# Softmax of four heads in one tile, one multiplication by the reciprocal sums, and FFN activations at another address

## The chip, the cores and the metric

One Trainium2 chip, of which the kernel uses one core. The metric is the time of one execution on the device in microseconds (us), the median of several runs. The engines are named as the profile names them: PE is TensorE (PEld its weight loads), DVE is VectorE, ACT is ScalarE, POOL is GpSimd, SP is SyncE, which issues the transfers.

## The reference

The program chains two stacks of layers on one sequence of 256 tokens of width 1024. The first stack has two layers (a recurrent mixer, a gated linear attention, each with a convolutional FFN). The second, which the change touches, has four layers; each is FFN, mixer, FFN, with a LayerNorm behind each of the three. The mixers are DSA, FoX, MLA and DSA again, all with 16 heads and causal softmax. Cut to what matters:

```
for i in range(4):
    x = layer_norm(ALPHA * x + 0.5 * swiglu(x, ffn1_w13[i], ffn1_w2[i]), ...)
    y = (dsa, fox, mla)[i % 3] mixer of x      # softmax attention, 16 heads, then @ w_out[i]
    x = layer_norm(ALPHA * x + y, ...)
    x = layer_norm(ALPHA * x + 0.5 * swiglu(x, ffn2_w13[i], ffn2_w2[i]), ...)

p = softmax(where(mask, q @ k.T * scale, -inf))   # per head
o = p @ v
```

DSA makes its mask with an indexer: eight small heads, a relu of their products, a weighted sum, and the 64 best keys of each query.

## The kernel before

Every product of an activation with a weight runs as three matmuls in fp32r: both are split into a high and a low part (`hi`, `lo`), and hi x hi, hi x lo, lo x hi are added up in PSUM (`mm_b`, lines 438 to 440: the activation is the stationary operand, 512 columns of weights move; `mm_a`, lines 445 to 447: the weight is stationary, 256 tokens move). Weights come from HBM in pieces of 512 KB; ACT casts the high part (line 371), DVE subtracts it for the low part (line 372).

In the second stack the tokens lie in two halves of 128, t = 0 and 1, each a Python generator that yields after every piece of weights. They run interleaved, and both use a piece while it is there. Tile's scheduler, from its own estimate of each instruction's duration and not by hand, sets the order in which each engine's instructions stand; each engine then works its list in that order. The middle part of an FFN (`ffn_both`) takes both halves at once.

An attention (`attend`) handles one group g of four heads of one half; four groups, two halves and four layers make 32 of them. Half 1 sees 256 keys, half 0 sees 128 (nk). The steps:
- line 1221: PE makes the scores of the four heads in two PSUM banks.
- line 1226: DVE adds the mask, scales and takes the maximum of each head (in the trace a custom instruction and a read of its accumulator); line 1228: ACT takes exp with that maximum as bias, in place in the head's tile `s`, with the row sum in one column of `sm`.
- line 1231: DVE takes the reciprocal `rc` of the four sums; line 1233: one multiplication by a scalar for each head.
- line 1240: PE transposes the probabilities in blocks of 128x128; line 1241: DVE copies the first two heads' transposes to `pT`, ACT the other two's; line 1248: PE multiplies with `v`.
- `split` (lines 450 and 451) makes `oThi` and `oTlo`, the stationary operands of the output projection, which follows when all four groups of a half are through (`groups`). While half 1 is still in its attentions, the output projection of half 0 is what PE has to do in between. It ends in half 0's LayerNorm (`ln`, lines 1075 to 1084: residual sum, statistics, aggregate, normalise, scale and shift; the reciprocal root `rstd` comes from POOL, lines 420 and 423).

Other users of the names that are touched: `hidden` (lines 1105 to 1108) makes the FFN's gated activation in `th`, which is split or transposed and split into `hT` (`ht`, from the tag kT), the stationary operand of the down projection; `dsa_index` makes the relu of the indexer in `rl`. `s`, `th` and `rl` share the tag `s1k`, with five buffers of 1 KB per partition. `pad` allocates a tile that nobody uses, to move the addresses behind it.

Of the kernel before, what the change touches and what calls it, by code (L numbers as in the profile page):

```python
# [8 lines left out]
F32 = mybir.dt.float32  # L9
F32R = mybir.dt.float32r  # L10
I32 = mybir.dt.int32
AF = mybir.ActivationFunctionType
OP = mybir.AluOpType
# [240 lines left out]
class _Cols:  # L254
    def __init__(self):
        self.at, self.parts, self.n = {}, [], 0
# [794 lines left out]
class Block2:  # L1051
    def __init__(self, k):
        self.k, self.nc, self.a, self.P, self.Q = k, k.nc, k.a, k.P, k.Q
        self.V, self.ACT = k.nc.vector, k.nc.scalar
        self.padded = False
        self.gbt, self.shared, self.v, self.vt = {}, {}, [None, None], {}

    def gb(self, i):
# [43 lines left out]
    def hidden(self, u, v, n):  # L1102

        V = self.V
        th = self.Q.tile([128, n], F32, name="th", tag="s1k", bufs=5)
        self.ACT.activation(out=th, in_=u, func=AF.Tanh, scale=0.5)
        V.scalar_tensor_tensor(out=th, in0=th, scalar=1.0, in1=u, op0=OP.add, op1=OP.mult)
        V.tensor_tensor(out=th, in0=th, in1=v, op=OP.mult)  # L1108
        return th

    def ht(self, key, c):

        if not self.hT:
            self.k.pad(self.Q, "h", 24)
        if (key, c) not in self.hT:
            self.hT[key, c] = self.Q.tile([128, 2, 2, 256], F32R, name="hT", tag="kT", bufs=4)
        return self.hT[key, c]
# [93 lines left out]
    def attend(self, t, g, qh, kh, v, mask, scale, oT):  # L1211


        k, Q, V, ACT, nc = self.k, self.Q, self.V, self.ACT, self.nc
        nk = 128 * (t + 1)
        sm = k.small("sm", 4)

        sp = [k.bank("u", 4, (128, 2, 256)) for _ in range(2)]
        scores = [sp[e % 2][:, e // 2, :nk] for e in range(4)]
        for e in range(4):  # L1220
            nc.tensor.matmul(scores[e], qh(e), kh(e), start=True, stop=True)  # L1221
        probs = []
        for e in range(4):
            s = Q.tile([128, 256], F32, name="s", tag="s1k", bufs=5)[:, :nk]
            nb = k.small(f"nb{e}")
            V.tensor_tensor_reduce(out=s, in0=scores[e], in1=mask[:, :nk], scale=-scale, scalar=3.0e38,
                                   op0=OP.add, op1=OP.min, accum_out=nb)
            ACT.activation(out=s, in_=s, func=AF.Exp, scale=-1.0, bias=nb, accum_out=sm[:, e:e + 1])
            probs.append(s)
        rc = k.small("rc", 4)  # L1230
        V.reciprocal(out=rc, in_=sm)
        for e in range(4):
            V.tensor_scalar(out=probs[e], in0=probs[e], scalar1=rc[:, e:e + 1], scalar2=None, op0=OP.mult)
        pTs = []
        for e0 in (0, 2):
            pt = k.bank("u", 4, (128, 2, 2, 128))
            pT = Q.tile([128, 2, 2, 128], F32, name="pT", tag="pT", bufs=2)
            for e in range(2):
                for j in range(t + 1):
                    nc.tensor.transpose(pt[:, e, j, :], probs[e0 + e][:, j * 128:j * 128 + 128], k.ident)  # L1240
            (ACT.copy if e0 else V.tensor_copy)(out=pT[:, :, :t + 1, :], in_=pt[:, :, :t + 1, :])
            pTs.append(pT)

        op = k.bank("u", 4, (128, 2, 128))
        for e0 in (0, 2):
            for j in range(t + 1):
                for e in range(2):
                    nc.tensor.matmul(op[e * 64:e * 64 + 64, e0 // 2, :], v[j][:, e0 + e, :], pTs[e0 // 2][:, e, j, :],  # L1248
                                     start=j == 0, stop=j == t)
        if not oT:  # L1250
            if not self.padded:
                k.pad(Q, "o", 16)
                self.padded = True
            oT += [Q.tile([128, 8, 128], F32R, name=f"oT{p}", tag=f"oT{p}{t}", bufs=1) for p in ("hi", "lo")]
        k.split(oT[0][:, g * 2:g * 2 + 2, :], oT[1][:, g * 2:g * 2 + 2, :], op)

# [36 lines left out]
    def dsa_index(self, t, i, xT):  # L1293

        k, Q, V, ACT, nc = self.k, self.Q, self.V, self.ACT, self.nc
        sh = self.shared.setdefault(i, {})
        nk = 128 * (t + 1)
        if t == 0:
            sh["kiT"] = Q.tile([128, 256], F32, name="kiT", tag="kiT", bufs=1)
        kiT = sh["kiT"]  # L1300
        ki = Q.tile([128, 2, 64], F32, name="ki", tag="ki", bufs=2)
        wi = Q.tile([128, 8], F32, name="wi", tag="wi", bufs=2)
        qi = Q.tile([128, 8, 64], F32, name="qi", tag="s2k", bufs=2)
        r = []
        for q, nm in enumerate("si"):
            yield from self.proj(t, f"mx{i}.{nm}", xT, 8, r)
            ACT.copy(out=qi[:, q * 4:q * 4 + 4, :], in_=r[q][:, :256].rearrange("p (h d) -> p h d", h=4))
            if q == 0:
                ACT.copy(out=ki[:, 0, :], in_=r[0][:, 256:320])
                self.rope(t, ki[:, 0:1, :16], 8, 0)  # L1310
                V.tensor_copy(ki[:, 1, :], ki[:, 0, :])
            else:
                ACT.activation(out=wi, in_=r[1][:, 256:264], func=AF.Copy, scale=8.0 ** -0.5)
        self.rope(t, qi[:, :, :16], 8, 0)
        p = k.bank("u", 4)
        nc.tensor.transpose(p[:, :128], ki.rearrange("p a d -> p (a d)"), k.ident)
        ACT.copy(out=kiT[:, t * 128:t * 128 + 128], in_=p[:, :128])
        qiT = Q.tile([128, 4, 128], F32, name="qiT", tag="s2k", bufs=2)
        self.transposes(qi.rearrange("p (a b) d -> p a (b d)", b=2), 4, 128, qiT)
        sc = Q.tile([128, nk], F32, name="sc", tag=f"sc{t}", bufs=1)  # L1320
        for h in range(8):
            if h % 4 == 0:
                dp = [k.bank("u", 4, (128, 2, 256)) for _ in range(2)]
                for q in range(4):
                    r = slice(q % 2 * 64, q % 2 * 64 + 64)
                    nc.tensor.matmul(dp[q % 2][:, q // 2, :nk], qiT[r, (h + q) // 2, :], kiT[r, :nk], start=True, stop=True)
            rl = Q.tile([128, 256], F32, name="rl", tag="s1k", bufs=5)
            ACT.activation(out=rl[:, :nk], in_=dp[h % 2][:, h % 4 // 2, :nk], func=AF.Relu, scale=0.125)
            if h == 0:
                V.tensor_scalar(out=sc[:, :nk], in0=rl[:, :nk], scalar1=wi[:, 0:1], scalar2=None, op0=OP.mult)  # L1330
            else:
                V.scalar_tensor_tensor(out=sc[:, :nk], in0=rl[:, :nk], scalar=wi[:, h:h + 1], in1=sc[:, :nk], op0=OP.mult, op1=OP.add)
        cm = self.cmask[:, 128 - t * 128:256]
        V.tensor_tensor(out=sc[:, :nk], in0=sc[:, :nk], in1=cm, op=OP.add)
        for r in range(8):
            m8 = k.small("m8", 8)
            V.max(out=m8, in_=sc[:, :nk])
            V.match_replace(out=sc[:, :nk], in_to_replace=m8, in_values=sc[:, :nk], imm_value=-3.0e30)
        mask = Q.tile([128, nk], F32, name="dmask", tag=f"dm{t}", bufs=1)
        V.tensor_scalar(out=mask[:, :nk], in0=sc[:, :nk], scalar1=-2.0e30, scalar2=NEG, op0=OP.is_ge, op1=OP.mult)  # L1340
        V.tensor_tensor(out=mask[:, :nk], in0=mask[:, :nk], in1=cm, op=OP.add)
        return mask
# [226 lines left out]
```

## Time and profile before

| | us |
|---|---|
| median of 3 runs | 2665.33 (2660.8 to 2668.5) |
| the profiled execution, its own time | 2664.02 |
| its span, first to last instruction | 2662.2 |
| PE busy | 2598.1 |
| DVE busy | 1919.3 |
| ACT busy | 1413.6 |

The times of rows are us from the start of the span. PE's matmuls overlap, so a matmul's own duration (0.39 us for 512 columns) is longer than the distance from its start to the next one's (0.23 us); the second is what PE takes for it. The granted clock of PE was 0.995 over the span, its upper level.

### The profile page before, as it was taken

How to read it: one execution, taken by the hardware profiler on the slowest of the kernel's cores; microseconds unless marked ns; L12 is line 12 of the kernel's file. 1: busy time of each engine (PE TensorE's matmuls, PEld its weight loads, DVE VectorE, ACT ScalarE, POOL GpSimd, SP SyncE). 2: the span in 40 equal slices, each digit the busy share in tenths (PEclk: the TensorE clock that was granted, in tenths of full speed). 3: DMA queues.
4: the chain of work that ended last, by engine and by line, in shares of the span. 5: the costliest groups of instructions: out<-in, count | busy, mean ns of one | idle time of the engine just before them, and what ended most of it. 6: DMA issues, size and time to landing. Idle time of an engine off the chain costs nothing.

```text
span 2662.2 us, 44260 instructions
## 1 busy us (share of the span) xinstructions
PE 2598.1 (98%) x16680; PEld 2287.7 (86%) x16680; DVE 1919.3 (72%) x3876; ACT 1413.6 (53%) x2848; POOL 75.3 (3%) x115
## 2 busy tenths in 40 slices
PE   7899999999999999999999999999999999999998
PEld 5688977899899778989987899899889989977897
DVE  6889879887666877576666856766885676687765
ACT  4565564765544655445456544544654454456542
POOL 0000010000000000000000000000000000000000
PEclk9999999999999999999999999999999999999999
DMA  8868764664664536656654565664445565453652
GB/s 317 297 230 293 243 226 164 224 217 159 225 191 151 183 122 226 191 184 206 193 179 125 183 192 180 214 190 154 166 163 194 183 206 190 160 182 126 213 191 96
DMA packets 141081, 514.39 MB, mean 193 GB/s; under 512 B 16177, under 2 KB 16561, under 8 KB 139330
## 3 DMA queue, kind: packets, MB, share of 16 engines
q1 hardware_dynamic: 140866, 511.56, 57.9%
q8 instruction: 131, 2.15, 0.3%
q14 instruction: 84, 0.69, 0.1%
HBM read 510.44 MB, written 1.05 MB: 192 GB/s over the span
## 4 chain that ended last, share of the span: by engine, by line
PE 78%; issue 8%; DVE 7%; DMA 3%; ACT 2%; POOL 1%; DVEq 0%; SPq 0%; POOLq 0%; ACTq 0%
PE u L445 11%; PE u L446 11%; PE u L447 11%; PE y L438 10%; PE y L440 10%; PE y L439 10%; PE u L438 3%; PE u L439 3%; PE u L440 3%; DVE lo L372 2%; DMA raw<-w 2%; DMA adar<-ada 1%; PE u L1221 1%; PE u L469 1%; PE u L1248 1%
## 5 line engine op out<-in xcount | busy, mean ns | idle before, releaser
L372 DVE TENSOR_TENSOR lo<-raw,hi 128x512 fp32r<-128x512 f32 (+4 forms) x1501 | 1081.1, 746 | 497.0 <-ACT hi L371 484.5
L371 ACT CAST hi<-raw 128x512 fp32r<-128x512 f32 (+4 forms) x1501 | 952.1, 667 | 730.3 <-issue 413.5
L445 PE MATMUL u<-hThi,hi 128*128 128x256 f32 x3016 | 840.1, 279 | 2.4 <-ACT hi L371 1.4
L447 PE MATMUL u<-hThi,lo 128*128 128x256 f32 x3016 | 837.0, 278 | 0.6 <-DVE lo L372 0.6
L446 PE MATMUL u<-hTlo,hi 128*128 128x256 f32 x3016 | 837.5, 278 | 0.0
L445 PEld LDWEIGHTS u<-hThi,hi 128*128 128x128 f32 x3016 | 567.7, 188 | 7.1 <-DVE mn L916 1.6
L446 PEld LDWEIGHTS u<-hTlo,hi 128*128 128x128 f32 x3016 | 567.6, 188 | 4.7 <-issue 1.0
L447 PEld LDWEIGHTS u<-hThi,lo 128*128 128x128 f32 x3016 | 569.1, 189 | 1.2 <-DVE lo L372 1.0
L440 PE MATMUL y<-hi,hT 128*128 128x512 f32 x704 | 278.2, 395 | 0.0
L438 PE MATMUL y<-hi,hT 128*128 128x512 f32 x704 | 277.8, 395 | 0.0
L439 PE MATMUL y<-lo,hT 128*128 128x512 f32 x704 | 277.7, 394 | 0.0
L438 PE MATMUL y<-hi,hThi 128*128 128x512 f32 (+6 forms) x504 | 190.1, 378 | 3.5 <-ACT hThi L450 3.3
L439 PE MATMUL y<-lo,hThi 128*128 128x512 f32 (+6 forms) x504 | 186.3, 371 | 0.1
L440 PE MATMUL y<-hi,hTlo 128*128 128x512 f32 (+6 forms) x504 | 185.3, 372 | 0.2 <-DVE hTlo L451 0.2
L440 PEld LDWEIGHTS y<-hi,hT 128*128 128x128 f32 x704 | 132.6, 188 | 30.7
L438 PEld LDWEIGHTS y<-hi,hT 128*128 128x128 f32 x704 | 132.6, 188 | 28.3
L439 PEld LDWEIGHTS y<-lo,hT 128*128 128x128 f32 x704 | 132.6, 188 | 28.3
L438 PE MATMUL u<-hi,hThi 128*128 128x512 f32 x320 | 126.9, 398 | 4.9 <-ACT hThi L450 4.9
L450 ACT CAST hT<-th 128x256 fp32r<-128x256 f32 x144 | 58.4, 405 | 130.5 <-DVE th L1108 130.5
L439 PE MATMUL u<-lo,hThi 128*128 128x512 f32 x320 | 125.4, 393 | 0.0
L440 PE MATMUL u<-hi,hTlo 128*128 128x512 f32 x320 | 124.1, 394 | 0.0
L438 PEld LDWEIGHTS y<-hi,hThi 128*128 128x128 f32 x504 | 95.2, 189 | 21.4 <-ACT hThi L450 5.1
(301 smaller groups left out, 3119.3 us busy)
## 6 DMA issues: line engine op xcount, KB each, us to landing
raw<-w SPq DMA_DIRECT2D x823, 512.0 KB, 3.9
adar<-ada SPq DMA_DIRECT2D x80, 512.0 KB, 4.9
gb<-lngb SPq DMA_DIRECT2D x12, 1024.0 KB, 4.9
adag<-ada SPq DMA_DIRECT2D x8, 512.0 KB, 5.7
adag<-adag SPq DMA_DIRECT2D x8, 512.0 KB, 6.0
raw<-w SPq DMA_DIRECT2D x8, 384.0 KB, 2.9
raw<-w SPq DMA_DIRECT2D x5, 480.0 KB, 3.6
raw<-w SPq DMA_DIRECT2D x4, 396.0 KB, 2.9
```

The source lines that it names most:

```text
L371: nc.scalar.copy(out=hi[:, a:b], in_=r[:, a:b])
L372: nc.vector.tensor_tensor(out=lo[:, a:b], in0=r[:, a:b], in1=hi[:, a:b].bitcast(F32), op=OP.subtract)
L438: mm(out, xhi, w[0], start=start, stop=False)
L439: mm(out, xhi, w[1], start=False, stop=False)
L440: mm(out, xlo, w[0], start=False, stop=stop)
L445: mm(out, whi, xhi, start=start, stop=False)
L446: mm(out, whi, xlo, start=False, stop=False)
L447: mm(out, wlo, xhi, start=False, stop=stop)
L450: self.nc.scalar.copy(out=hi, in_=src)
L469: self.nc.tensor.transpose(p[:, k * 128:k * 128 + 128], x[:, (h + k) * 128:(h + k + 1) * 128], self.ident)
L1221: nc.tensor.matmul(scores[e], qh(e), kh(e), start=True, stop=True)
L1248: nc.tensor.matmul(op[e * 64:e * 64 + 64, e0 // 2, :], v[j][:, e0 + e, :], pTs[e0 // 2][:, e, j, :], start=j == 0, stop=j == t)
```

## The change

The four tiles `s` of a head become one tile `s4` of four heads and nk keys for each half (tags s40 and s41, one buffer each); the heads' slices of it are what reductions, exp and transposes use. The four multiplications by a scalar become one multiplication of two tensors, in which `rc` is broadcast along the keys. The tag s1k keeps `th` and `rl` and has two buffers. The pad ahead of `hT` shrinks from 24 to 8 floats and the pad ahead of `oT` is gone.

```diff
     def hidden(self, u, v, n):
-        th = self.Q.tile([128, n], F32, name="th", tag="s1k", bufs=5)
+        th = self.Q.tile([128, n], F32, name="th", tag="s1k", bufs=2)
...
     def ht(self, key, c):
         if not self.hT:
-            self.k.pad(self.Q, "h", 24)
+            self.k.pad(self.Q, "h", 8)
...
-        probs = []
+        s4 = Q.tile([128, 4, nk], F32, name="s", tag=f"s4{t}", bufs=1)
+        probs = [s4[:, e, :] for e in range(4)]
         for e in range(4):
-            s = Q.tile([128, 256], F32, name="s", tag="s1k", bufs=5)[:, :nk]
             nb = k.small(f"nb{e}")
-            V.tensor_tensor_reduce(out=s, in0=scores[e], in1=mask[:, :nk], scale=-scale, scalar=3.0e38,
+            V.tensor_tensor_reduce(out=probs[e], in0=scores[e], in1=mask[:, :nk], scale=-scale, scalar=3.0e38,
                                    op0=OP.add, op1=OP.min, accum_out=nb)
-            ACT.activation(out=s, in_=s, func=AF.Exp, scale=-1.0, bias=nb, accum_out=sm[:, e:e + 1])
-            probs.append(s)
+            ACT.activation(out=probs[e], in_=probs[e], func=AF.Exp, scale=-1.0, bias=nb, accum_out=sm[:, e:e + 1])
         rc = k.small("rc", 4)
         V.reciprocal(out=rc, in_=sm)
-        for e in range(4):
-            V.tensor_scalar(out=probs[e], in0=probs[e], scalar1=rc[:, e:e + 1], scalar2=None, op0=OP.mult)
+        V.tensor_tensor(out=s4, in0=s4, in1=rc[:, :, None].to_broadcast([128, 4, nk]), op=OP.mult)
...
         if not oT:
-            if not self.padded:
-                k.pad(Q, "o", 16)
-                self.padded = True
...
-            rl = Q.tile([128, 256], F32, name="rl", tag="s1k", bufs=5)
+            rl = Q.tile([128, 256], F32, name="rl", tag="s1k", bufs=2)
```

The addresses in a partition follow from the sizes of the tiles in the order of their first use. Modulo 256 bytes, the weights `hi` and `lo` stay at 224 and the activations `hThi` and `hTlo` at 160; `hT` goes from 96 to 32, `oThi` and `oTlo` from 224 to 96.

The order of the engines changes inside the four mixers only; those of the FFNs and of the first stack are as they were. In the changed kernel lines 1057 to 1220 are one lower, and the attention's are 1220 (scores), 1225, 1227 (exp), 1229 (reciprocal), 1231 (multiplication), 1238, 1239, 1246. The transposes of 1240 stand in 32 rows of PE's order in place of 50, the products of 1248 in 33 rows in place of 40.

DVE at the last attention (g = 3) of half 1 in layer 0, before, from the last reduction on; `x_70` is half 0's residual stream, `dmask` the mask:

```order
L1226 ISA s,nb_10152<-u,dmask 128x256
L1226 ISA nb_10152 128x1
L1075 SCALAR_TENSOR_TENSOR x_70<-x_70,y 128x512 x2
L1231 RECIPROCAL rc<-sm 128x4
L1076 BN_STATS bnst<-x_70 128x6
L1233 TENSOR_SCALAR s<-s,rc 128x256 x4
L1076 BN_STATS bnst<-x_70 128x6
L1241 COPY pT<-u 128x512
L1078 BN_AGGR bnmv<-bnst 128x2
```

The same place on DVE, after:

```order
L1225 ISA s,nb_10106<-u,dmask 128x256
L1225 ISA nb_10106 128x1
L1077 BN_AGGR bnmv<-bnst 128x2
L1080 SCALAR_TENSOR_TENSOR x_70<-x_70,bnmv,gb 128x1024
L1229 RECIPROCAL rc<-sm 128x4
L1083 SCALAR_TENSOR_TENSOR x_70<-x_70,rstd,gb 128x512
L1231 TENSOR_TENSOR s<-s,rc 128x1024
L1083 SCALAR_TENSOR_TENSOR x_70<-x_70,rstd,gb 128x512
L372 TENSOR_TENSOR lo_10336<-raw,hi_10335 128x512
L1239 COPY pT<-u 128x512
```

The residual sums and statistics of half 0 (1075 and 1076) have moved ahead of the reductions, and the aggregate, the normalisation and half of the scaling stand between the reductions and the multiplication.

PE at the same place, before, from the last matmuls of the output projection ahead of the transposes on:

```order
L438 MATMUL y<-hi_10051,oThi 128x512
L439 MATMUL y<-lo_10052,oThi 128x512
L1240 MATMUL u<-ident,s 128x128 x2
L440 MATMUL y<-hi_10051,oTlo 128x512
L1240 MATMUL u<-ident,s 128x128 x6
L438 MATMUL y<-hi_10051,oThi 128x512
L439 MATMUL y<-lo_10052,oThi 128x512
L440 MATMUL y<-hi_10051,oTlo 128x512
L438 MATMUL y<-hi_10196,oThi 128x512
L1248 MATMUL u<-pT,v 64x128 x8
```

And after:

```order
L438 MATMUL y<-hi_10147,oThi 128x512
L439 MATMUL y<-lo_10148,oThi 128x512
L440 MATMUL y<-hi_10147,oTlo 128x512
L1238 MATMUL u<-ident,s 128x128 x8
L1246 MATMUL u<-pT,v 64x128 x8
L469 MATMUL u<-ident,x_70 128x128 x4
L438 MATMUL y<-hi_10167,oThi 128x512
```

Between the scores and the first transpose stood 17 matmuls of the output projection and now stand 15; between the transposes and the products with v stood four and now none.

DVE at the attention g = 2 of half 1 in the MLA layer, before, from the last reduction on:

```order
L1226 ISA s,nb_20661<-u,cmask 128x256
L1226 ISA nb_20661 128x1
L1231 RECIPROCAL rc<-sm 128x4
L1233 TENSOR_SCALAR s<-s,rc 128x256 x4
L1075 SCALAR_TENSOR_TENSOR x_70<-x_70,y 128x512
L1241 COPY pT<-u 128x512
```

And after:

```order
L1225 ISA s,nb_20525<-u,cmask 128x256
L1225 ISA nb_20525 128x1
L1074 SCALAR_TENSOR_TENSOR x_70<-x_70,y 128x512
L1075 BN_STATS bnst<-x_70 128x6
L1229 RECIPROCAL rc<-sm 128x4
L1077 BN_AGGR bnmv<-bnst 128x2
L372 TENSOR_TENSOR lo_20811<-raw,hi_20810 128x512
L1231 TENSOR_TENSOR s<-s,rc 128x1024
L1080 SCALAR_TENSOR_TENSOR x_70<-x_70,bnmv,gb 128x1024
L1239 COPY pT<-u 128x512
```

A residual sum, statistics, an aggregate and a low part have come ahead of the multiplication, and the normalisation ahead of the copy. On PE there stood 13 matmuls of the output projection between these scores and the first transpose, and now 7; five stood between the transposes and the products with v, and now none.

## Rows read from the trace of the kernel before

**Rows 1.** The page: busy time by engine, and the chain that ended last, by engine.
```profile
PE 2598.1 (98%) x16680; PEld 2287.7 (86%) x16680; DVE 1919.3 (72%) x3876; ACT 1413.6 (53%) x2848; POOL 75.3 (3%) x115
PE 78%; issue 8%; DVE 7%; DMA 3%; ACT 2%; POOL 1%; DVEq 0%; SPq 0%; POOLq 0%; ACTq 0%
```
**Rows 2.** What PE waited for: line, waited for, us in total, times, longest.
```profile
PE u L1240 <- DVE s L1233: 4.6, 6, 1.8
```
**Rows 3.** Groups of PE's matmuls: line, tiles, shape, count, busy, mean ns, idle.
```profile
L440 PE MATMUL y<-hi,hT 128*128 128x512 f32 x704 | 278.2, 395 | 0.0
...
L438 PE MATMUL y<-hi,oThi 128*128 128x512 f32 x128 | 52.9, 414 | 0.0
```
**Rows 4.** PE's timeline: first and last matmul of an hT and an hThi stretch.
```profile
835.33 0.39 PE L438 MATMUL y<-hi,hT 128*128 128x512 f32 x1
...
857.40 0.39 PE L440 MATMUL y<-hi,hT 128*128 128x512 f32 x1
...
2156.63 0.40 PE L439 MATMUL u<-lo,hThi 128*128 128x512 f32 x1
...
2166.71 0.40 PE L438 MATMUL u<-hi,hThi 128*128 128x512 f32 x1
```
**Rows 5.** Groups on DVE, by shape: count, busy us, mean ns, idle before.
```profile
L1233 DVE TENSOR_SCALAR s<-s,rc 128x256 f32<-128x256 f32 x64 | 18.2, 349 | 0.4
L1233 DVE TENSOR_SCALAR s<-s,rc 128x128 f32<-128x128 f32 x64 | 14.0, 282 | 0.5
...
L372 DVE TENSOR_TENSOR lo<-raw,hi 128x512 fp32r<-128x512 f32 x1291 | 849.9, 686 | 463.3 <-ACT hi L371 452.8
L372 DVE TENSOR_TENSOR lo<-raw,hi 128x1024 fp32r<-128x1024 f32 x180 | 217.9, 1219 | 33.7 <-ACT hi L371 31.7
```
**Rows 6.** Timelines of DVE (first row) and PE, layer 0, half 1, g = 3.
```profile
984.50 0.42 DVE L1226 CUSTOM_DVE_ANT_0 s<-u,dmask 128x256 f32<-128x256 f32 x1 [1.39 <-PE u L1221]
...
984.40 0.50 PE L438 MATMUL y<-hi,oThi 128*128 128x512 f32 x1
984.75 0.40 PE L439 MATMUL y<-lo,oThi 128*128 128x512 f32 x1
...
988.21 0.39 PE L439 MATMUL y<-lo,oThi 128*128 128x512 f32 x1
988.56 0.41 PE L1240 MATMUL u<-ident,s 128*128 128x128 f32 x2
```
**Rows 7.** PE's timeline right behind them, around the products of pT and v.
```profile
990.40 0.40 PE L438 MATMUL y<-hi,oThi 128*128 128x512 f32 x1
990.73 1.09 PE L1248 MATMUL u<-pT,v 128*64 128x128 f32 x16
991.75 0.50 PE L439 MATMUL y<-lo,oThi 128*128 128x512 f32 x1
992.09 0.40 PE L440 MATMUL y<-hi,oTlo 128*128 128x512 f32 x1
```
**Rows 8.** Timelines of DVE and PE, MLA layer, half 1, g = 3; idle in brackets.
```profile
1950.43 0.42 DVE L1226 CUSTOM_DVE_ANT_0 s<-u,cmask 128x256 f32<-128x256 f32 x1
...
1954.18 0.75 DVE L1084 SCALAR_TENSOR_TENSOR x<-x,rstd,gb 128x512 f32<-128x512 f32 x1 [0.67 <-POOL rstd L423]
1954.85 1.14 DVE L1233 TENSOR_SCALAR s<-s,rc 128x256 f32<-128x256 f32 x4
...
1953.16 0.39 PE L440 MATMUL y<-hi,oTlo 128*128 128x512 f32 x1
1955.35 1.15 PE L1240 MATMUL u<-ident,s 128*128 128x128 f32 x8 [1.80 <-DVE s L1233]
```
**Rows 9.** The same in the MLA layer at g = 2.
```profile
1940.01 0.42 DVE L1226 CUSTOM_DVE_ANT_0 s<-u,cmask 128x256 f32<-128x256 f32 x1 [1.72 <-PE u L1221]
...
1942.81 1.14 DVE L1233 TENSOR_SCALAR s<-s,rc 128x256 f32<-128x256 f32 x4
...
1943.31 1.15 PE L1240 MATMUL u<-ident,s 128*128 128x128 f32 x8
```

More of the change, by code (lines that the diff above doesn't have):

```diff
@@ L1054, in __init__ @@
         self.V, self.ACT = k.nc.vector, k.nc.scalar
-        self.padded = False
         self.gbt, self.shared, self.v, self.vt = {}, {}, [None, None], {}
```

## The prediction

> **What bounds the kernel now.** I read the page first: TensorE (PE) is busy for 98% of the span and holds 78% of the chain that ended last, so time moves only where PE gets slower steps, fewer steps, or a wait [rows 1]. Next the list of what PE waited for: at the changed place, L1240 (transposes of the probabilities) behind DVE's normalisation L1233, it lost 4.6 us in 6 waits, the longest 1.8 us [rows 2]. So there is little waiting to win; the question is what new waiting appears, and whether PE's steps change. For the steps I read start to start along PE's timeline, since the busy time of overlapping matmuls does not give it.
>
> **PE's step and the address of hT.** The FFN activations hT are the stationary operand of 3 x 704 matmuls with 512 moving columns [rows 3]. From 835.33 to 857.40 us there are 95 steps on hT: 22.07 / 95 = 232.3 ns each. From 2156.63 to 2166.71 there are 44 steps on hThi: 10.08 / 44 = 229.1 ns [rows 4]. The moving operand is the same kind in both, weights at 224 modulo 256 bytes; hT starts at 96 modulo 256, hThi at 160.  I ascribe the 3 ns to the address and expect hT at 32 modulo 256, the mirror image of 160 around 224, to step like hThi. No fp32r stationary operand of the kernel before lies at 32, so the price has bounds only: at best the 3.2 ns between the rows, 2112 x 3.2 ns = 6.8 us; at worst 0, since hT stands now in the slowest class that the trace shows (a loss is not excluded by that, but nothing points to a class slower still). I take 2.8 ns, a little under the difference, because oThi at 224 lies between the two: **-5.9 us**. The attention outputs oThi and oTlo go the other way, 224 to 96: 3 x 128 = 384 matmuls [rows 3]. Their 15 steps from 984.75 to 988.21 take 3.46 / 15 = 230.7 ns [rows 6], the class 96 takes 232.3; 384 x 1.6 ns = 0.6, **+0.7 us** with the few steps of that class in the MLA layer that are faster still.
>
> The Trainium skill, "TensorE: Matmul & The Clock Gate", Part 2, says that loading the next weights takes no read bandwidth from the running matmul, the two reads having ports of their own. By that rule the residue moves nothing and both terms above are 0. The trace speaks against it as far as 3 ns can, no row shows residue 32, and so this is the first rival.
>
> **The normalisation.** Removed: 64 multiplications of 128x256 (349 ns) and 64 of 128x128 (282 ns) on DVE. Added: 16 of 128x1024 and 16 of 128x512 with one operand broadcast. No row of before has that operation; nearest are the subtractions of L372 of the same size, 1219 and 686 ns [rows 5], which I take, since a broadcast read is no extra tensor. Sum removed 32.2 us busy, added 16 x 1.22 + 16 x 0.69 = 30.5 us: nothing, and DVE has 28% idle. What counts is the chain: PE may begin to transpose after the first of four multiplications now, and only after the whole one then. For half 1, before: 1942.81 to 1943.31, 0.50 us [rows 9]; after: 1.22 + the same 0.15 us of handover = 1.37 us, so +0.87. For half 0: 0.69 - 0.28 = +0.40.
>
> Of the 32 attentions 27 lie in the middle of a mixer. There the order puts 2 more matmuls (half 0) or 4 more (half 1) between scores and transposes: 0.46 and 0.92 us at 0.23. The longer chain is thus covered by other PE work, with 0.05 us to spare each. Of the waits of [rows 2] that are not the one at 1955.35, 2.8 us, a part goes: I take **-1.0 us**, between -1.7 (0.06 x 27) and +3 (a tenth of a microsecond uncovered each).
>
> **Fewer switches on PE.** The order after has the pT times v matmuls of L1248 in 33 runs instead of 40. A run costs on entry 990.40 to 990.73 = 0.33 in place of 0.23, and on leaving 991.75 to 992.09 = 0.34 in place of 0.23 [rows 7]: 0.2 x 7 = 1.4, **-1.4 us**. Transposes in one piece rather than two I cost at nothing: a switch inside them shortens one neighbour by about what it adds to the other.
>
> **The last attention of half 1 in each layer.** Here the price is. The fill for these waits is half 0's out-projection, and the new order has used more of it up by then; and half 0's LayerNorm, whose first part is ready sooner, now stands on DVE between the reductions and the normalisation. In the layers 0, 1 and 3 (groups g = 3) the order after runs: reductions, BN_AGGR, L1080 over 1024, reciprocal, one L1083, the multiplication. L1083 needs rstd from POOL. The trace has this DVE order once, at 1950.43 in the MLA layer: from the first reduction to the multiplication takes 1954.85 - 1950.43 = 4.42 us, 0.67 of it waiting for POOL [rows 8]. With 1.37 to the first transpose it makes 5.79 us. In layer 0 before, the reduction began at 984.50 and the transposes at 988.56, 4.06 us, behind 17 matmuls [rows 6]. After there are 15: 0.35 for the first and 14 x 0.23 from 984.40 end at 987.97, and 0.10 for the switch makes 988.07, 3.57 us after the first reduction (17 by the same sum give 988.53). Stall: 5.79 - 3.57 = 2.2 us. Then nothing stands between transposes and L1248 any more, where 4 matmuls stood. The copy of pT on DVE waits behind the second L1083 (0.67) and a lo (0.60): 1.22 + 0.67 + 0.60 + 0.68 = 3.17 us after the multiplication began, while the transposes end at 1.37 + 1.15 = 2.52: stall 0.65. So 2.9 x 3 = 8.7 us. In the MLA layer g = 2 goes from 13 matmuls of fill to 7, and L1075, L1076 and a lo, three operations of 512 columns at some 0.6, come ahead of the multiplication: 1.47 for the reductions, 1.8 for these, 0.35 for reciprocal and BN_AGGR, 1.37 to the transposes, 5.0 us after the first reduction, against 0.35 + 6 x 0.23 + 0.1 = 1.85 of fill: 3.1, and 0.6 for the copy. At g = 3 DVE is relieved of the LayerNorm, but there are 7 matmuls of fill there too: 1942.81 - 1940.01 = 2.80 to the multiplication as in rows 9, 4.17 to the transposes, 2.3 of stall against the 1.96 lost there now (1953.16 + 0.23 to 1955.35, rows 8): +0.4, and +0.3 for its copy. Together 4.4. **+13.1 us**. Lower bound: if rstd comes without a wait and the LayerNorm finds DVE idle while ACT's exp runs, each of the four is up to 1.5 us cheaper, some +7.
>
> Edits costed at nothing: th and rl with 2 buffers instead of 5. A new tanh waits for the use of the one two back, which lies a whole up-projection of 24 x 0.23 = 5.5 us earlier; relu is paced by DVE's accumulation already. If that cover fails, up to 1 us in each of the two DSA layers. s4 has one buffer per half; two attentions of a half are over 7 us apart. No transfer moves, and POOL's order stays.
>
> **Sum:** -5.9 + 0.7 - 1.0 - 1.4 + 13.1 = +5.5. The profiled execution took 2664.0, so 2669.5; the median of the three runs is 2665.3, 1.3 above the profiled one, within their spread. A measurement here can tell about 0.3%, 8 us: faster is below 2657.3, slower above 2673.3.
>
> **Rivals.** (1) Slower: the address gives nothing while the layer ends cost in full: -1.0 - 1.4 + 13.1 = +10.7, 2674.7. It decides at a step on hT that stays above 231.5 ns. For it: residue 32 is inferred, no row has it; against: two classes of address with steady steps, each in stretches of quite different work. It is also where the Trainium skill's rule above leads. (2) Faster: the layer ends cost next to nothing, because the early LayerNorm lets the next FFN of half 0 start without a wait, giving back what was lost: -7.6 and 0 to 3 on top, 2656.4 to 2659.4. For it: PE's total work is the same and the order was laid out with these chains known; against: after these places the trace of before has hardly a wait to give back. (3) Both terms fail to appear, the waits are hidden and the step stays: -1.0 - 1.4 = -2.4, 2661.6.
>
> **How the numbers follow.** Forecast case 0.52, 2663 to 2673; rival 1 0.22; rival 2 0.16; rival 3 0.10. Rival 1 lies close to the slower bound, and the forecast case's upper tail adds a little: slower 0.24. Of rival 2 most is under the faster bound: 0.13. The rest is the same. The range 2657 to 2677 takes in all of the forecast, most of rivals 1 and 3, and cuts rival 2.
>
> **What would show it.** hT stretches at 229 to 230 ns a step; oThi at 232; the multiplication at 1.2 and 0.7 us; waits of L1238 on it in the list of PE's waits of some 9 us in 4 or 5 places at the layer ends, 2 to 3 us each, and of L1246 on pT some 2 to 3 us; none of weight in the middle of a mixer. Wrong would be: hT still at 232, or a multiplication that is dearer than the subtraction, which adds its surplus to all 32 chains, or stalls of th or rl on ACT.

## The result, and the profile after

The changed kernel takes 2687.5 us (2685.2 to 2690.9, 4 runs) against 2665.5 us in the runs beside it: 1.0087 times as long, 95% interval 1.0074 to 1.0100. It is slower by 22 us; the forecast was 2669.5, the range ended at 2677. The profiled execution of after took 2690.9 us, 26.9 more than that of before, so its parts add up to somewhat more than the medians differ by.

The page of the changed kernel, busy time and the chain by engine, as [rows 1]:

```profile
PE 2610.0 (97%) x16680; PEld 2300.8 (86%) x16680; DVE 1922.9 (72%) x3780; ACT 1414.0 (53%) x2848; POOL 76.0 (3%) x115
...
PE 79%; issue 7%; DVE 7%; DMA 3%; ACT 2%; POOL 1%; DVEq 0%; SPq 0%; POOLq 0%; ACTq 0%
```

PE is busy for 12 us more with the same 16680 instructions: its steps got slower. The span grew by 27, so some 15 us are new idle time. The list of PE's waits names most of that, as [rows 2] (L1238 are the transposes, L1231 the one multiplication, L1246 the products with v):

```profile
PE u L1238 <- DVE s L1231: 10.9, 6, 3.1
...
PE u L1238 <- ACT hi L371: 3.8, 3, 1.9
...
PE u L1246 <- DVE pT L1239: 3.2, 5, 0.7
```

Together 17.9 us, where the same two places had 4.9 before. The transposes do not read `hi`; the second row is their wait too, put down to what came last, with the 1.9 us at the end of layer 1.

The multiplication itself costs what was expected; groups on DVE, as [rows 5]:

```profile
L1231 DVE TENSOR_TENSOR s<-s,rc 128x1024 f32<-128x1024 f32 x16 | 19.6, 1223 | 0.4
...
L1231 DVE TENSOR_TENSOR s<-s,rc 128x512 f32<-128x512 f32 x16 | 11.1, 691 | 0.4
```

Where the time went is seen best by cutting PE's timeline at the middle parts of the second stack's eight FFNs: each runs from the first of its five stretches of 96 matmuls of L445 to L447 to the end of its closing stretch of 288, with hT stretches of 24 between them. The table gives, for each profiled execution, the sum over the eight middle parts, over the four mixers (from the end of one middle part to the start of the next, with the FFN ends around the mixer) and over the three joints between the layers with the tail up to PE's last matmul, in us:

| | before | after | after - before |
|---|---|---|---|
| up to the first middle part | 719.9 | 720.9 | +0.9 |
| eight FFN middle parts | 922.2 | 930.0 | +7.8 |
| four mixers with their surroundings | 780.7 | 798.4 | +17.7 |
| three joints of FFN and FFN, and the tail to the last matmul | 230.6 | 231.0 | +0.4 |

The FFNs, which were forecast to win, lose. On hT, as [rows 4], 95 steps from the first to the last matmul of the same stretch in the changed kernel:

```profile
837.24 0.39 PE L438 MATMUL y<-hi,hT 128*128 128x512 f32 x1
...
859.40 0.39 PE L440 MATMUL y<-hi,hT 128*128 128x512 f32 x1
```

22.16 / 95 = 233.3 ns instead of 232.3. And beside it a thing that no term of the prediction had: a stretch of 96 matmuls of 256 columns between two hT stretches, with operands of its own that did not move. Before, its first and last matmul:

```profile
753.28 0.28 PE L445 MATMUL u<-hThi,hi 128*128 128x256 f32 x1
...
764.06 0.28 PE L447 MATMUL u<-hThi,lo 128*128 128x256 f32 x1
```

And after:

```profile
754.27 0.28 PE L445 MATMUL u<-hThi,hi 128*128 128x256 f32 x1
...
765.46 0.28 PE L447 MATMUL u<-hThi,lo 128*128 128x256 f32 x1
```

10.78 us before, 11.19 after: 113.5 ns a step against 117.8. Before, only the first of an FFN's five such stretches was slow; after, the first, third and fifth are. Two more in each of eight FFNs make 16 x 0.42 = 6.7 us; the hT steps within the middle parts are about the rest of the 7.8.

The mixers lose at the layer ends, where it was forecast, and more than that. Layer 0, half 1, g = 3 in the changed kernel, DVE (the rows that answer to [rows 6] and to [rows 8]):

```profile
989.52 0.20 DVE L1077 BATCH_NORM_AGGREGATE bnmv<-bnst 128x2 f32<-128x12 f32 x1
989.76 1.28 DVE L1080 SCALAR_TENSOR_TENSOR x<-x,bnmv,gb 128x1024 f32<-128x1024 f32 x1
990.96 0.17 DVE L1229 RECIPROCAL rc<-sm 128x4 f32<-128x4 f32 x1
991.80 0.75 DVE L1083 SCALAR_TENSOR_TENSOR x<-x,rstd,gb 128x512 f32<-128x512 f32 x1 [0.67 <-POOL rstd L423]
992.47 1.22 DVE L1231 TENSOR_TENSOR s<-s,rc 128x1024 f32<-128x1024 f32 x1
```

and PE there:

```profile
990.98 0.39 PE L440 MATMUL y<-hi,oTlo 128*128 128x512 f32 x1
993.83 1.27 PE L1238 MATMUL u<-ident,s 128*128 128x128 f32 x8 [2.46 <-DVE s L1231]
995.61 1.98 PE L1246 MATMUL u<-pT,v 128*64 128x128 f32 x16 [0.51 <-DVE pT L1239]
997.52 1.12 PE L469 MATMUL u<-ident,x 128*128 128x128 f32 x4
998.28 0.78 PE L438 MATMUL y<-hi,oThi 128*128 128x512 f32 x1
998.86 0.63 PE L439 MATMUL y<-lo,oThi 128*128 128x512 f32 x1
999.28 0.63 PE L438 MATMUL y<-hi,oThi 128*128 128x512 f32 x1
```

The gap ahead of the transposes is 993.83 - 990.98 = 2.85 us where 0.35 stood. But read on: the 16 products with v take 1.98 us, where [rows 7] have 1.09, and the matmuls of the output projection behind them stand 0.42 us apart instead of 0.23. The stretches of the same places by window (us, busy time and instructions of PE, PEld, DVE, ACT, POOL, then the granted clock PEclk, DMA share, GB/s):

```profile
991.00:993.80 2.80, 0.37 (x2) 0.00 (x0) 2.13 (x5) 2.80 (x6) 0.68 (x2) 1.00 0.00 0
...
995.60:997.50 1.90, 1.89 (x16) 1.57 (x16) 1.76 (x3) 0.18 (x1) 0.00 (x0) 0.50 0.38 34
...
998.50:1000.00 1.50, 1.50 (x5) 1.21 (x5) 1.27 (x3) 0.58 (x1) 0.00 (x0) 0.50 0.86 325
```

Behind the gap the granted clock fell to its lower level, 0.50, and stayed there for some 7 us. PE pays for the wait, and then for the work behind it.

### The profile page after: what moved, and what is told of

It is laid out like the page before. It is cut to its first block, busy times and chain, and to the rows that moved or that the text cites. A ratio compares the mean times of both kernels' runs of the same rounds, so it can differ in the third digit from the quotient of the medians.

```text
span 2689.1 us, 44264 instructions
## 1 busy us (share of the span) xinstructions
PE 2610.0 (97%) x16680; PEld 2300.8 (86%) x16680; DVE 1922.9 (72%) x3780; ACT 1414.0 (53%) x2848; POOL 76.0 (3%) x115
## 4 chain that ended last, share of the span: by engine, by line
PE 79%; issue 7%; DVE 7%; DMA 3%; ACT 2%; POOL 1%; DVEq 0%; SPq 0%; POOLq 0%; ACTq 0%
PE u L447 11%; PE u L445 11%; PE u L446 11%; PE y L438 11%; PE y L440 11%; PE y L439 11%; PE u L438 3%; PE u L439 3%; PE u L440 3%; DVE lo L372 2%; DMA raw<-w 2%; DMA adar<-ada 1%; PE u L469 1%; PE u L1246 1%; PE u L1220 1%
## 5 line engine op out<-in xcount | busy, mean ns | idle before, releaser
L371 ACT CAST hi<-raw 128x512 fp32r<-128x512 f32 (+4 forms) x1501 | 951.3, 667 | 720.9 <-PE u L446 213.6
L445 PE MATMUL u<-hThi,hi 128*128 128x256 f32 x3016 | 841.9, 279 | 3.2 <-ACT hi L371 2.0
L447 PE MATMUL u<-hThi,lo 128*128 128x256 f32 x3016 | 839.2, 278 | 0.2 <-DVE lo L372 0.2
L445 PEld LDWEIGHTS u<-hThi,hi 128*128 128x128 f32 x3016 | 567.1, 188 | 7.8 <-ACT hi L371 2.2
L447 PEld LDWEIGHTS u<-hThi,lo 128*128 128x128 f32 x3016 | 567.6, 188 | 0.6 <-DVE lo L372 0.4
```

The costliest lines, as they stand in the source:

```text
L371: nc.scalar.copy(out=hi[:, a:b], in_=r[:, a:b])
L445: mm(out, whi, xhi, start=start, stop=False)
L447: mm(out, wlo, xhi, start=False, stop=stop)
```

## The experiments

Theory A, formed from the two traces: two causes that add up, the address of hT (all of the FFNs' 8 us) and the gaps at the layer ends. That the clock takes a part of its own was seen only when e5 came out faster than either of its theories had it. Rivals: the two buffers of th and rl, the shared tile, or the length of the one multiplication by itself. The order of every engine was kept wherever possible, so that an experiment moves one thing: in the traces it is that of the changed kernel in e1, and that of the kernel before in e2, e4, e7, e8 and e10 to e12.

**e1: the changed kernel with hT back at 96.** The indexer's small tile wi, two buffers of 32 bytes, is allocated ahead of hT and not behind it, which moves hT by 64 bytes.

```diff
             self.k.pad(self.Q, "h", 8)
+            self.Q.tile([128, 8], F32, name="wi", tag="wi", bufs=2)
```

> The changed kernel with hT back at residue 96 modulo 256 (the small tile wi is allocated ahead of it); every engine's order is as in the changed kernel. Theory A, that the address of hT costs the FFNs about 9.5 us (1.8 on hT's own steps, 7.7 on the 256-column matmuls beside them): about 2678 us, hT steps at 232.3 ns, the 96-matmul stretches of L445 to L447 nearly all at 10.78 us. Rival B, that the FFNs lose by the two buffers of th and not by the address: 2687 us, as the changed kernel.

Measured: 2679.1 us, ratio 1.0053 (1.0039 to 1.0067). hT steps at 232.3 ns, the eight middle parts at 922.2 us in sum, exactly as before; the mixers still at 798.3. The address is the FFNs' whole loss, and none of the mixers'.

**e2: the kernel before with hT at 32.**

```diff
-            self.k.pad(self.Q, "h", 24)
+            self.k.pad(self.Q, "h", 8)
...
-                k.pad(Q, "o", 16)
+                k.pad(Q, "o", 32)
```

> The kernel before with hT at residue 32 instead of 96 (pads of 8 and 32 floats for 24 and 16; oT stays at 224); orders as before. Theory A: +9.5 us, about 2675 us, hT at 233.2 ns and every second 96-matmul stretch at 11.19 us instead of 10.78. Rival B: 2665.5 us, as before.

Measured: 2676.4 us, ratio 1.0039 (1.0025 to 1.0054); hT at 233.2 ns, stretches alternating, middle parts 930.0 us. Nothing but the pads differs from the kernel before, so rival B is out. Of the tiles that a middle part uses (raw, hi, lo, th, the activations at 160 and hT) the pads move hT alone. Its stretch, 838.67 to 860.83 for 95 steps, is that of after:

```profile
838.67 0.39 PE L438 MATMUL y<-hi,hT 128*128 128x512 f32 x1
...
860.83 0.39 PE L440 MATMUL y<-hi,hT 128*128 128x512 f32 x1
```

**e3: e1 with four multiplications by a scalar on the shared tile.**

```diff
-        V.tensor_tensor(out=s4, in0=s4, in1=rc[:, :, None].to_broadcast([128, 4, nk]), op=OP.mult)
+        for e in range(4):
+            V.tensor_scalar(out=probs[e], in0=probs[e], scalar1=rc[:, e:e + 1], scalar2=None, op0=OP.mult)
```

> As e1 (one tile for four heads, two buffers for th and rl, hT at 96, oT at 96), but with the four multiplications by a scalar instead of the one. The order falls back to nearly that of before. Theory A, that the one multiplication and the order it brings cost some 14 us at the layer ends: about 2666 us, no wait over 2 us of the transposes except the one that the kernel before has. Rival C, that the shared tile or the buffers cost it: about 2678 us, as e1.

Measured: 2665.1 us, ratio 0.9999 (0.9989 to 1.0009). The shared tile, the two buffers and oT's address cost nothing that can be measured; the one multiplication, or the order that comes with it, costs all of the 14 us.

**e4: the kernel before with hT at 160.** Pads of 40 and 0 floats.

```diff
-            self.k.pad(self.Q, "h", 24)
+            self.k.pad(self.Q, "h", 40)
...
-                k.pad(Q, "o", 16)
```

> The kernel before with hT at residue 160 (pad of 40 floats ahead of hT, none ahead of oT, which stays at 224). If the step depends on the residue of the stationary operand alone, hT steps at 229.3 ns as hThi does there: 2112 x 3.0 ns = 6.3 us less, about 2659 us. If what counts is the rhythm in which a stretch is entered, the steps may stay at 232 and the time at 2665, and the 256-column stretches may change instead, up to 8 us either way.

Measured: 2657.8 us, ratio 0.9977 (0.9966 to 0.9989): faster than both kernels. 95 steps from 834.53 to 856.27, 228.8 ns:

```profile
834.53 0.39 PE L438 MATMUL y<-hi,hT 128*128 128x512 f32 x1
...
856.27 0.40 PE L440 MATMUL y<-hi,hT 128*128 128x512 f32 x1
```

So an address of hT can give what the prediction hoped for; 32 is just not one that does.

**e5: e1, but the last attention of half 1 in each layer with four multiplications again.** The order stays nearly that of the changed kernel at the layer ends, LayerNorm first and 15 or 7 matmuls of fill; only the copy of pT moves ahead of the second L1083 on DVE, and PE makes the products with v in two runs of eight.

```diff
+        if t == 0 or g < NG - 1:
             V.tensor_tensor(out=s4, in0=s4, in1=rc[:, :, None].to_broadcast([128, 4, nk]), op=OP.mult)
+        else:
+            for e in range(4):
+                V.tensor_scalar(out=probs[e], in0=probs[e], scalar1=rc[:, e:e + 1], scalar2=None, op0=OP.mult)
```

> As e1, but the last attention (g = 3) of half 1 in each layer has the four multiplications by a scalar again; the other 28 keep the one. The order at the layer ends stays as in the changed kernel: LayerNorm of half 0 ahead of the normalisation on DVE, 15 matmuls (7 in the MLA layer) of fill on PE and none behind the transposes. Theory A1, that the order costs there and the multiplication's length only 0.87 us of it: e1 less 4 x 0.9, about 2675.5 us; gap ahead of the transposes at the end of layer 0 about 2.0 us instead of 2.85. Theory A2, that the length of the one multiplication costs: about 2666 us.

Measured: 2670.1 us, ratio 1.0019 (1.0011 to 1.0028), between the two theories. The gap at the end of layer 0 is what A1 said, 988.70 - 986.71 = 1.99 us; PE there:

```profile
986.71 0.39 PE L440 MATMUL y<-hi,oTlo 128*128 128x512 f32 x1
988.70 1.15 PE L1243 MATMUL u<-ident,s 128*128 128x128 f32 x8 [1.60 <-DVE s L1236]
990.11 0.66 PE L1251 MATMUL u<-pT,v 128*64 128x128 f32 x8 [0.26 <-DVE pT L1244]
```

The gaps sum to 4.4 us less than in e1, as A1 had it within one microsecond. What A1 lacked is in the windows of the same stretch:

```profile
989.00:991.00 2.00, 1.74 (x17) 1.12 (x16) 1.98 (x5) 1.17 (x3) 0.00 (x0) 1.00 0.04 12
991.00:993.00 2.00, 2.00 (x17) 1.51 (x16) 1.74 (x4) 0.95 (x2) 0.00 (x0) 1.00 0.05 16
```

Behind the gap of 2.0 us the clock stayed at 1.00 in this execution; in e1, behind the gap of 2.9 us at the same place, it was 0.50:

```profile
987.00:989.00 2.00, 1.88 (x10) 1.58 (x10) 1.99 (x4) 0.13 (x1) 0.00 (x0) 0.50 0.03 8
989.00:991.00 2.00, 2.00 (x21) 1.67 (x20) 1.74 (x3) 0.96 (x2) 0.00 (x0) 0.74 0.34 55
```

Summed over windows of 2 us from 715 us to the end of the last mixer, what the clock took away (one minus the granted clock, times 2 us) is 0 in before, 10.2 us in after, 11.9 in e1, 1.7 in e3, e5 and e6. Of the difference of e5 to e1, 9.0 us by the medians, 4.4 are gaps; the other 4.6 lie well within the 10.2 by which the clock's loss differs. That the clock takes them is argued from these sizes, since no run changes the clock alone. The loss is not that of the profiled executions only: the mean granted clock was 0.990 to 0.992 in all five executions of e1, and 0.992 to 0.995 in the eleven of e5.

**e6: the reverse, the one multiplication only in those last attentions.** The condition of e5 with `t == 1 and g == NG - 1`.

> As e1, but only the last attention of half 1 in each layer has the one multiplication, the other 28 the four. The order then has 21 or 22 matmuls ahead of the transposes at the ends of the layers 0, 1 and 3 and four behind them, and no aggregate or L1080 ahead of the multiplication there. Theory A1: the longer multiplication is covered, no gap over 0.6 us there but the one of the MLA layer's end (2.2 before, about 3 now): about 2667 us. Theory A2: 3 x 2.5 + 0.9 us of gaps at the layer ends, about 2674 us.

Measured: 2665.7 us, ratio 1.0002 (0.9993 to 1.0012): A1. PE at the end of layer 0, with the same 1.2 us multiplication, but 21 matmuls ahead and neither the aggregate nor the normalisation and scaling of the LayerNorm in its way:

```profile
988.71 0.39 PE L440 MATMUL y<-hi,oTlo 128*128 128x512 f32 x1
988.97 1.06 PE L1243 MATMUL u<-ident,s 128*128 128x128 f32 x8
```

No gap. At the end of the MLA layer, where the transposes waited already in the kernel before (2.19 us from matmul to transpose, [rows 8]), the length shows: 3.00 us.

```profile
1955.20 0.40 PE L440 MATMUL y<-hi,oTlo 128*128 128x512 f32 x1
1958.20 1.06 PE L1243 MATMUL u<-ident,s 128*128 128x128 f32 x8 [2.60 <-DVE s L1233]
```

So the length of the one multiplication costs nothing where other matmuls cover it. In the order that the scheduler lays out when all 32 attentions have it, it is not covered: shortening it at four places (e5, with the small shifts of order named there) wins back 9.0 of the 14 us. The loss needs both, an order that leaves too little fill and the length that then lies open.

**e7, e8, e10, e11, e12: the other residues of hT,** in the kernel before, one execution each, with pads as e2 and e4 and oT at 224 throughout.

> The kernel before with hT at residue 224, that of the weights (pads of 56 and 48 floats). By the steps of oThi, which stands there in the kernel before: 230.2 ns, 4.4 us less than before, about 2660 us. If a class that is entered from another one steps in another rhythm, no number holds; 228 to 233 ns.

> The kernel before with hT at residue 192 (pads of 48 and 56 floats), between the 160 of e4 (229.0 ns) and 224. If the step varies smoothly with the distance to the weights' residue, 229 to 230 ns and about 2658 us; if it is set by multiples of 64 bytes apart, as 96, 160, 224 and 32 all are from one another, 192 is a class of its own that nothing predicts: 226 to 236 ns.

> The kernel before with hT at residue 0 (no pad ahead of hT, 40 floats ahead of oT). Known by now: 229.0 ns at 160, 226.7 at 224, 232.3 at 96, 233.2 at 32, 233.4 at 192. If residues an odd multiple of 64 bytes plus 32 form a family (32, 96, 160, 224) and the others another, 0 goes with 192: 233 to 235 ns a step, stretches all at 11.19 us, about 2690 us. If 192 was alone: 229 to 233, 2660 to 2676 us.

> The kernel before with hT at residue 128 (pads of 32 and 8 floats). By the family of e8 (192): about 233 ns and 2690 us; by nearness to 96 and 160: 229 to 232 ns and 2658 to 2665 us.

> The kernel before with hT at residue 64 (pads of 16 and 24 floats). By the family of e8 (192): about 233 ns and 2690 us; by nearness to 32 and 96: 232 to 233 ns and 2665 to 2676 us.

Measured; the step is the mean over the intervals between neighbouring hT matmuls in stretches of 24 and more, the stretch is from the first to the last start of L445 to L447:

| hT modulo 256 | run | hT step, ns | 96-matmul stretches, us | eight middle parts, us | time, us |
|---|---|---|---|---|---|
| 0 | e10 | 233.2 | 10.78, all | 919.8 | 2669.6 (one execution) |
| 32 | e2 | 233.2 | 11.19 and 10.78 in turn | 930.0 | 2676.4 |
| 64 | e12 | 234.0 | 10.8, the first 11.19 | 924.6 | 2662.5 (one execution) |
| 96 | before | 232.3 | 10.78, the first 11.19 | 922.2 | 2664.2 |
| 128 | e11 | 233.3 | 10.8, all | 920.7 | 2664.0 (one execution) |
| 160 | e4 | 229.0 | 10.8, all | 916.4 | 2657.8 |
| 192 | e8 | 233.4 | 11.19, all | 946.7 | 2690.6 (one execution) |
| 224 | e7 | 226.7 | 11.19, all | 940.3 | 2676.9 (one execution) |

Neither the family of e8's text nor nearness predicts this. 224 has the fastest hT steps of all and is slow, because it holds all the 256-column stretches, the closing ones of 288 matmuls too, in the slow rhythm. At 32 most steps are 231 or 236 ns, at 224 nearly all are 226 or 227. The column of the middle parts repeats to 0.1 us between executions with the same address (930.0 in after and e2, 922.2 in before, e1 and e3); the single times carry the scatter of one run.

**e9: e2 with another entry into the stretches.** The last three 512-column matmuls ahead of each 96-matmul stretch as six of 256 columns.

```diff
                         for t in range(2):
-                            self.ff_down(t, key, d, kk, n, w)
+                            if t and n and kk and d == _ff_downs(c)[-1]:
+                                for q in range(2):
+                                    z = slice(q * 256, q * 256 + 256)
+                                    h = self.hT[key, d]
+                                    k.mm_b(self.y[key][t][n][:, z], h[:, kk, 0, 128:], h[:, kk, 1, 128:], (w[0][:, z], w[1][:, z]), False, False)
+                            else:
+                                self.ff_down(t, key, d, kk, n, w)
```

> As e2 (hT at 32), but the last three 512-column matmuls of the down projection ahead of each 96-matmul stretch of L445 to L447 are issued as six of 256 columns; same work, same addresses. Theory E, that the rhythm of a stretch is set by how it is entered: the stretches no longer alternate 10.78 and 11.19 us as in e2. Rival F, that hT's address acts throughout the stretch: they alternate as in e2, about 2676 us.

Measured: 2672.0 us in one execution; the stretches take 11.19, 10.79, 11.19, 10.79, 11.19 us, as in e2. The width of three matmuls at the entry does not change the rhythm.

That does not make rival F right, though. PE does not read hT in such a stretch; ACT and DVE write it then, but late. In the changed kernel a slow stretch begins at 754.27 and the next, fast one at 771.18; their 25th matmuls, and the first write of hT in the slow one:

```profile
757.10 0.28 PE L445 MATMUL u<-hThi,hi 128*128 128x256 f32 x1
...
761.95 0.40 ACT L450 CAST hT<-th 128x256 fp32r<-128x256 f32 x1
...
771.18 0.28 PE L445 MATMUL u<-hThi,hi 128*128 128x256 f32 x1
...
773.92 0.28 PE L445 MATMUL u<-hThi,hi 128*128 128x256 f32 x1
```

24 steps take 2.83 us in the one and 2.74 in the other, long before hT is touched, 7.7 us in. In all 14 traces, 40 stretches each, every step from the seventh on is 112 to 115 ns in a fast stretch and 116 to 120 in a slow one, and hT is never written earlier than 7.4 us in. So the address cannot act throughout the stretch. What remains is what touches hT ahead of it, the hT matmuls before all, and at 32 the last step into a stretch agrees: in the changed kernel it is 229 or 230 ns ahead of all 24 slow stretches and 235 or 236 ahead of all 16 fast ones, in e9 (256 columns) 113 or 114 and 117 or 118. (In the kernel before the two kinds are not so far apart: 234 or 235 and 232 to 234.) The rhythm thus stands at the entry, as theory E has it, and e9 changed the width of the entry but not the address read there. How that address sets it was not found, and stays open.

## Why the prediction was wrong

**hT's address, -5.9 us: the step that failed, in sign.** The argument took two classes of address, 96 and 160, and put 32 with 160 because both lie 64 from the weights. e2 shows +0.9 ns a step instead of -2.8, 2112 x 0.9 = +1.9 us, and the table shows that no such symmetry exists. The bound was wrong as well: that 96 was "the slowest class that the trace shows" was true and no bound, since five of the other seven are slower. And the edit was costed on hT's own matmuls alone; its larger part, 6.7 us, is on the 256-column matmuls between them, whose addresses no part of the change touches. From -5.9 to +8 makes some 14 of the 21 us by which the profiled executions miss the sum (+26.9 against +5.5).

The Trainium skill, "TensorE: Matmul & The Clock Gate", Part 2, says that loading the next weights takes no read bandwidth from the running matmul. Taken as the prediction took it, that the address moves nothing, it does not hold here either: 226.7 to 234.0 ns by the address of hT alone. Whether the two reads get in each other's way no run shows.

**oT, +0.7: right.** From 988.19 to 990.98 the changed kernel's oT steps are 2.79 / 12 = 232.5 ns, 230.7 before; e3 shows that it can't be seen in the time.

**The one multiplication and its chain, 0: right; the middle attentions, -1.0: half of it.** 1223 and 691 ns were forecast as 1219 and 686. The gaps ahead of the transposes of the 27 middle attentions sum to 12.0 us before and 11.5 after, -0.5 (the lower bound given for them, 0.06 x 27, is 1.6 and not 1.7); the order covers the longer chain as reckoned. **Fewer switches, -1.4:** the entries into L1248 of the same attentions sum to 9.7 before and 8.8 after, -0.9; the leaving was not measured, so the size is near but not shown.

**The layer ends, +13.1: the gaps right to half a microsecond, their price not; the second step that failed.** Gaps ahead of the transposes, after less before: layer 0 2.50 (forecast 2.2), layer 1 2.07, MLA g = 2 3.17 (3.1), g = 3 0.50 (0.4), layer 3 2.50; ahead of L1246 0.60, 0.66, 0.60, 0.40, 0.65: 13.6 us in all. Yet the mixers lose 17.7. What the sum lacked is the clock: a gap was costed as its own length, while the gaps here are 2.3 to 3.5 us long, and behind four of the five the clock fell to 0.50. In layer 0 the work from L1246 to the second set of transposes of x takes 5.93 us in after (995.61 to 1001.54), nearly all of it at 0.50, 3.91 in e1 (988.99 to 992.90), which had only part of it at the low clock, and 3.73 in e5 (990.11 to 993.84), which had none: 2.2 us for the clock at this place. The ends of the three, in this order:

```profile
1001.54 0.48 PE L438 MATMUL y<-hi,oThi 128*128 128x512 f32 x1
...
992.90 0.48 PE L438 MATMUL y<-hi,oThi 128*128 128x512 f32 x1
...
993.84 0.48 PE L438 MATMUL y<-hi,oThi 128*128 128x512 f32 x1
```

The 10.2 us that the clock took away are an upper bound of its cost; with the gaps they make 23.8, 6 more than the mixers lost; 1.4 of that are the gains of the middle attentions above, the rest is not assigned.

**The rivals.** Rival 1 had the sign and put the address at nothing, 2674.7; the address cost, and the clock came on top. Its point of decision, a step on hT above 231.5 ns, was the right thing to look at. Rivals 2 and 3, in which the layer ends cost next to nothing, are refuted by e1, which keeps all of the change but hT's address and is some 14 us slower than the kernel before. th and rl with two buffers cost nothing (e3).

## What to carry to other kernels

Price a stall on a busy TensorE twice: its own length, and the work behind it at the granted clock that the trace shows there. A scheduler's order is part of a change: in e6 the same operation at the ends of three layers costs nothing, so read what the new order puts between the producer and the wait, and how much fill is left at the ends of phases. When tiles change size, addresses move; record where each hot operand lies, keep them there while testing something else, and measure an address rather than infer it from its neighbours.

## What the runs showed of the hardware

The address of the stationary operand hT modulo 256 bytes moved the step of its 512-column fp32r matmuls between 226.7 and 234.0 ns, and the step of the 256-column matmuls that follow on them, with operands of their own, between 113.5 and 117.8 ns; such a stretch keeps to its end the step on which it settles within its first six matmuls or so; the best address for the first (224) is among the worst for the second. With the granted clock at 1.00 throughout, the eight FFN middle parts took 916 to 947 us by that address alone.

The granted clock fell to 0.50 for 3 to 7 us in or behind TensorE gaps of 2.1 to 3.5 us within otherwise full work, and not always. Behind the gap at the end of the MLA layer it stayed at 1.00 in after (2.69 us) and fell in e1 (2.59 us), which has the same order; in the ten executions where that gap is 2.1 to 2.2 us (before, e2 to e4, e7 to e12) it fell in four (e2, e3, e8, e11). Behind the four gaps of 1.3 to 2.0 us in e5 it did not fall. So the same order costs differently from one execution to the next.
